# One kernel, one change: plain weight layout in the feed-forward part, mLSTM with carried states, and other groups and steps

## The chip, the cores and the metric

The kernel runs on one core of a Trainium2 chip. It is one launch; the metric is the device time of that launch in microseconds, taken as the median of three runs. A core has engines that each work through a queue of their own: TensorE (PE in the profile; its weight loads are listed as PEld), VectorE (DVE), ScalarE (ACT), GpSimd (POOL), and SyncE (SP), which here only issues DMAs.

## The reference

One encoder layer over 512 tokens of width 1024, with a memory of 256 tokens. All is fp32.

```python
h = rms_norm(x)
proj = h @ w_in       # q,k,v,o,gates of the mLSTM | q,k,v of attention B | q of attention C | 3 merge gates
A = mlstm_branch(...)                     # 4 heads of 128, forward and backward scan, summed
B = neighbourhood_attention(...)          # 8 heads of 64 on an 8 x 64 grid
C = memory_cross_attention(...)           # 4 heads of 128 into rms_norm(mem)
x = x + (g_ml * (A @ w_br_ml) + g_na * (B @ w_br_na) + g_xa * (C @ w_br_xa)) @ w_out
x = x + (gelu(dwconv3(a)) * u) @ w_down   # a, u = split(rms_norm(x) @ w_up), 2816 wide each
return rms_norm(x)
```

The mLSTM of one direction is linear attention with decay: a step keeps a state `C` (128 x 128) and a normaliser `n` (128) and does `C = decay * C + wt * v k^T`; within a chunk the scores are `exp(D) * q k^T`, and the result is scaled by `1 / max(|den|, exp(-m))`. The reference uses chunks of 64 tokens; any chunk length gives the same sums.

## The kernel before

**Products.** Activations stand channel by token: `XH`, `XL` hold the normalised input as a high part (rounded to the fast fp32r format) and the rest. A weight block is loaded raw by SP (`emit_raw`, L153, 512 KB), and split by `emit_split`: ACT copies it into the high half of a tile `w` (L213), DVE subtracts to get the low half (L214). `mm3` (L229 to L231) is high x high, high x low, low x high, so a *product* of one block (8 tiles of the contraction, 512 tokens) is 24 matmuls of 128x512. Each block is two `w` tiles; four `w` tiles exist, so ACT and DVE prepare the block after the one that PE is working on.

**Layout of w.** `layout` and `form` say where the high and low halves lie in a `w` tile. All blocks but two kinds have the plain layout, (1, 0, 0): high half from column 0, low half from column 512. The 44 blocks of the feed-forward's up projection (`ua`, `uu`) go through the 22 entries of `FORMS` in turn: shifted by 16, 32 or 48 floats; high and low interleaved (step 2) or interleaved by four (step 4) at several shifts; and eight in which the token axis is read and written backwards. `dn` blocks (down projection) are plain.

**Stages.** mLSTM q and k (`mlq`, `mlk`); then the token-major groups `tm` (tokens are the stationary side, the weights move): gates and half of v (272 columns), the other half of v (256), and attention B's v in two groups of 256; then products for C's q (`xaq`), the output gate (`o`), memory keys and values (`memk`, `memv`), B's q and k, three branches of eight merge gates with the branch projections, `out`, and twice up and down.

**Attention beside products.** The three mixers are generators (`ml_all`, `xa_all`, `na_all`), advanced by `step` after products at 1.4 steps a product (0.75 in the shorter memory products, `RATE` in the gates, half of it after the fourth contraction tile and half after the product). What `step` emits goes to the engines with the products around it. The order in which instructions then stand on each engine is fixed when the program is built, by a scheduler that may move one past another; on the chip each engine takes its own in that order.

**The mLSTM before.** `ml_prep` makes running gate sums (`lf`, scans over 512 tokens), the maxima `mr` and row biases, writes them to DRAM (`rd`, L546) and `load_R` reads them back, spread over all partitions: `R[d]` for direction d, 256 KB each (L576, SP), and `rm[d]`, the same plus a triangle mask (L579, POOL). Four buffers hold R and rm of one head. Per head, `kq_part` makes all 512 x 512 scores with four `mm3` (48 matmuls of 128x512 in all four heads) and ACT moves them to SBUF (L588). `weights_J` makes, for each 128-token block J of queries, five 128x128 tiles `exp(R + bias)` on ACT (L598) and multiplies them with the scores on DVE (L599, L600): one for each earlier key block (direction 0), each later one (direction 1) and the two diagonal ones. `values_J` multiplies them with `va` (v with a column of ones, 129 columns) on PE (L610): 80 plain fp32 matmuls, which the trace lists as 160, two for each. Then come the normaliser and the head's norm (L612 to L628).

## Time and profile before

| | |
|---|---|
| median of three runs | 899.22 us (898.06 to 899.22) |
| the profiled execution | 899.35 us, of which the span from the first to the last instruction is 897.6 us |
| 51.6 to 98.1 us | token-major groups |
| 98.1 to about 250 us | C's q, output gate, memory, B's q and k, with the mLSTM beside them |
| about 250 to 440 us | merge gates and branch projections, with attentions C and B beside them |
| 520.6 to 644.8 and 704.7 to 827.5 us | up projections, 22 products each |
| 644.8 to 704.7 us | first down projection |

A few rows in the prediction are read as follows. A page line such as `PE 888.7 (99%) x4438` is busy time, share of the span and number of instructions. A row of windows gives a stretch, its length, the busy time of each engine with the number of its instructions, the granted clock, and the DMA share. A row of the timeline gives the start, the length, the engine, line, operation and tiles, and in brackets how long the engine had been idle and what ended that. PE's matmuls overlap in the rows: 0.39 us is the modelled length of one, and the distance from one start to the next is what it costs.

### The profile page before, as it was taken

What the parts mean: (1) busy time and instruction counts of PE and PEld (TensorE: products, weight loads), DVE (VectorE), ACT (ScalarE), POOL (GpSimd) and SP (SyncE); (2) the same over time, 40 slices, a digit from 0 to 9 for tenths busy, and PEclk for the clock granted to TensorE, in tenths of its full rate; (3) what the DMA queues carried; (4) which work ended last, traced back from release to release, by engine and by line L of the source; (5) the groups of instructions that cost most, each with busy time, mean ns of one, the idle gap of its engine ahead of it and who ended that gap; (6) DMA issues with size and microseconds to landing.
All of it is one profiled execution on the core that took longest, in us unless ns stands there. A gap on an engine that the chain in (4) does not pass through costs nothing.

```text
span 897.6 us, 12396 instructions
## 1 busy us (share of the span) xinstructions
PE 888.7 (99%) x4438; PEld 758.9 (85%) x4438; DVE 599.7 (67%) x1138; ACT 467.6 (52%) x982; POOL 158.0 (18%) x236
## 2 busy tenths in 40 slices
PE   8999999999999999999999999999999999999997
PEld 7899888988888888888888888898888888988897
DVE  6795567747666757998766657677733577777433
ACT  7474446656544647898734435554422344544442
POOL 4201221112070660420000212111100011111010
PEclk9999999999999999999999999999999999999999
DMA  7323633532242443443323432322233322222312
GB/s 251 108 78 131 191 127 118 164 95 94 71 119 94 117 123 125 136 135 118 118 94 106 140 107 80 109 93 95 65 103 96 113 94 95 94 93 89 114 58 94
DMA packets 39437, 99.69 MB, mean 111 GB/s; under 512 B 5960, under 2 KB 13640, under 8 KB 39376
## 3 DMA queue, kind: packets, MB, share of 16 engines
q1 hardware_dynamic: 31728, 92.45, 31.6%
q0 software_dynamic: 7360, 6.32, 3.3%
q8 instruction: 35, 0.57, 0.2%
q14 instruction: 26, 0.21, 0.1%
q10 hardware_dynamic: 288, 0.14, 0.1%
HBM read 94.67 MB, written 4.21 MB: 110 GB/s over the span
## 4 chain that ended last, share of the span: by engine, by line
PE 93%; ACT 2%; DMA 2%; DVE 2%; issue 1%; SPq 0%; POOL 0%; POOLq 0%; ACTq 0%; DVEq 0%
PE mm L229 27%; PE mm L231 27%; PE mm L230 27%; PE at L229 2%; PE at L231 2%; PE at L230 2%; PE at L610 2%; PE at L755 1%; DMA R<-rd 1%; PE at L736 1%; DMA wr<-wflat 1%; DMA rd<-s 0%; PE at L843 0%; ACT s L727 0%; PE at L717 0%
## 5 line engine op out<-in xcount | busy, mean ns | idle before, releaser
L229 PE MATMUL mm<-u,w 128*128 128x512 f32 (+1 forms) x1077 | 418.7, 389 | 1.1 <-ACT w L213 0.8
L230 PE MATMUL mm<-u,w 128*128 128x512 f32 (+1 forms) x1077 | 416.2, 386 | 0.1
L231 PE MATMUL mm<-u,w 128*128 128x512 f32 (+1 forms) x1077 | 416.2, 386 | 0.0
L213 ACT ACTIVATE w<-wr 128x512 fp32r<-128x512 f32 (+1 forms) x290 | 181.9, 631 | 239.1 <-PE mm L231 207.0
L214 DVE TENSOR_TENSOR w<-wr,w 128x512 fp32r<-128x512 f32 (+3 forms) x291 | 220.8, 760 | 116.7 <-ACT w L213 113.4
L231 PEld LDWEIGHTS mm<-u,w 128*128 128x128 f32 x1077 | 207.7, 193 | 39.8 <-DVE w L214 0.4
L229 PEld LDWEIGHTS mm<-u,w 128*128 128x128 f32 x1077 | 207.8, 193 | 39.4 <-ACT w L213 1.3
L230 PEld LDWEIGHTS mm<-u,w 128*128 128x128 f32 x1077 | 207.8, 193 | 38.8 <-DVE u L236 0.8
L1171 POOL TENSOR_TENSOR s<-s,rb 128x512 f32<-128x512 f32 x22 | 30.6, 1392 | 265.2 <-DVE s L1170 256.6
L482 POOL DMA_DIRECT2D u<-nav_d x128 | 62.3, 501 | 73.3 <-PE at L755 33.6
L235 ACT ACTIVATE u<-s 128x512 fp32r<-128x512 f32 x34 | 21.4, 630 | 53.9 <-DVE s L1174 52.2
L236 DVE SCALAR_TENSOR_TENSOR u<-s,u 128x512 fp32r<-128x512 f32 x34 | 23.5, 691 | 14.9 <-ACT u L235 14.7
L598 ACT ACTIVATE E<-R,bi 128x128 f32<-128x128 f32 x80 | 27.9, 395 | 7.8 <-POOL R L579 3.8
L1017 POOL TENSOR_TENSOR acc<-acc,s 128x512 f32<-128x512 f32 x7 | 9.1, 1296 | 128.8 <-ACT s L1016 128.8
L400 ACT ACTIVATE s<-pad,vec 128x512 f32<-128x512 f32 x30 | 24.4, 812 | 6.9 <-DVE pad L398 6.6
L401 DVE SCALAR_TENSOR_TENSOR s<-pad,vec,s 128x512 f32<-128x512 f32 x30 | 22.5, 750 | 3.5 <-ACT s L400 2.6
L229 PE MATMUL mm<-w,u 128*128 128x256 f32 (+1 forms) x80 | 24.7, 308 | 0.0
L1170 DVE SCALAR_TENSOR_TENSOR s<-s,s 128x512 f32<-128x512 f32 x22 | 15.2, 692 | 14.0 <-ACT s L1169 14.0
L231 PE MATMUL mm<-w,u 128*128 128x256 f32 (+1 forms) x80 | 24.4, 305 | 0.0
L230 PE MATMUL mm<-w,u 128*128 128x256 f32 (+1 forms) x80 | 24.3, 304 | 0.0
L402 DVE SCALAR_TENSOR_TENSOR s<-pad,vec,s 128x512 f32<-128x512 f32 x30 | 22.5, 750 | 0.7
L1169 ACT ACTIVATE s<-s 128x512 f32<-128x512 f32 x22 | 13.9, 632 | 17.0 <-DVE s L1168 16.9
(276 smaller groups left out, 1066.7 us busy)
## 6 DMA issues: line engine op xcount, KB each, us to landing
wr<-wflat SPq DMA_DIRECT2D x140, 512.0 KB, 3.4
s<-xT SPq DMA_DIRECT2D x16, 256.0 KB, 4.1
nab<-nabias SPq DMA_DIRECT2D x16, 256.0 KB, 2.7
u<-nav_d POOLq DMA_DIRECT2D x128, 32.0 KB, 2.5
wr<-wflat SPq DMA_DIRECT2D x15, 192.0 KB, 2.4
nav_d<-nv POOLq DMA_DIRECT2D x8, 256.0 KB, 3.5
R<-rd SPq DMA_DIRECT2D x8, 256.0 KB, 3.6
wr<-wflat SPq DMA_DIRECT2D x2, 544.0 KB, 3.4
```

The source lines that it names most:

```text
L213: A.activation(h[:, u:v], src, AF.Copy)
L214: V.tensor_tensor(l[:, u:v], src, h[:, u:v].bitcast(F32), op=ALU.subtract)
L229: PE.matmul(ps, lh, rh, start=start, stop=False)
L230: PE.matmul(ps, lh, rl, start=False, stop=False)
L231: st["mm"] = PE.matmul(ps, ll, rh, start=False, stop=stop).ins
L236: V.scalar_tensor_tensor(l, src, scale, h.bitcast(F32), op0=ALU.mult, op1=ALU.subtract)
L400: A.activation(t1, pad[:, 0:512], AF.Identity, scale=vcol(w, i), bias=vcol(b, i))
L401: V.scalar_tensor_tensor(t1, pad[:, 1:513], vcol(w, n + i), t1, op0=ALU.mult, op1=ALU.add)
L402: V.scalar_tensor_tensor(t1, pad[:, 2:514], vcol(w, 2 * n + i), t1, op0=ALU.mult, op1=ALU.add)
L482: G.dma_start(vw[r * 32:(r + 1) * 32, i * 256:(i + 1) * 256], nav_v[hf, r, CW[b]:CW[b] + 32, hp * 256:(hp + 1) * 256])
L598: A.activation(E[:, i, :], src, AF.Exp, bias=bi[:, d, abs(J - s), s, h:h + 1])
L1171: G.tensor_tensor(c, c, rb2, op=ALU.mult)
```

## The change

There are five parts.

1. `FORMS`, `layout` and `form` go; every `w` tile has the plain layout. The new small tiles (`dg`, `ex`, `en`, less `tot` and the smaller `bi`) take 64 more fp32 columns ahead of the `w` tiles, 256 bytes.
2. Token-major groups are 272, 512 and 256 columns wide: the second half of v and the first half of B's v share one group.
3. The mLSTM goes by chunks of 128 tokens with carried states. q and k are kept as plain fp32, one unit buffer each (no split by `split_act`), and the unit buffers are 14 for 15. `keys` makes only the four diagonal score blocks of a head (plain fp32, 128x128), transposes the four key blocks, and scales them into `kt` (direction 0 on ACT, direction 1 on DVE). `states` multiplies three scaled key blocks per direction with v and adds them up into `C`. `diagonal` makes the eight diagonal exp tiles, `queries` the six scaled query tiles, and `values_J` adds one diagonal and one state matmul per direction. `load_R` of the next head is called two steps earlier. E tiles are six of 4 x 128 for two of 5 x 128.
4. `step` is called once after the eighth tile of a gate product and once after a branch projection.
5. Attention B's transposed weights use the same E tiles.

```diff
-NU = 15
+NU = 14
+EB = 6
 WARM = 13
 RM, RB = 0.75, 1.4
-RATE = (0.85, 1.05, 1.2)
+TMW = (272, 512, 256)
...
-FORMS = tuple((1, 16 * i, 0) for i in range(4)) + tuple((2, 8 * i, 0) for i in range(8)) + ((4, 0, 0), (4, 16, 0)) \
-    + tuple((1, 16 * i, 1) for i in range(4)) + tuple((2, 16 * i, 1) for i in range(4))
...
-            e = w[:, at:at + 2 * m].rearrange("p (j x) -> p x j", x=2)
-            h, l = e[:, 0, :], e[:, 1, :]
-        elif step == 4:
-            e = w[:, at:at + 2 * m].rearrange("p (y j z x) -> p x y z j", y=2, x=2, z=2)
-            h, l = e[:, 0], e[:, 1]
-            return h, l, [(h[:, k // 2, k % 2], l[:, k // 2, k % 2]) for k in range(4)]
-        else:
...
-                parts = [(h[:, k * c:(k + 1) * c], l[:, k * c:(k + 1) * c]) for k in range(b - a)]
             else:
-                step, at, _ = layout(key)
                 w = wp.tile([P, WT], F32R, tag="w", name=nm("w"), bufs=4)
-                h, l, parts = form(w, step, at, m, c)
+                h, l = w[:, :m], w[:, 512:512 + m] if m <= 512 else w[:, WT - m:]
...
-            split[i].extend(parts)
+            for k in range(a, b):
+                q = slice((k - a) * c, (k - a + 1) * c)
+                split[i].append((h[:, q], l[:, q]))
...
-            if layout(key)[2]:
-                mm3(ps[:, ::-1], ws[k][0], ws[k][1], XHs[k][:, ::-1], XLs[k][:, ::-1], k == 0, k == KT - 1)
-            else:
-                mm3(ps[:, :n], ws[k][0], ws[k][1], XHs[k], XLs[k], k == 0, k == KT - 1)
+            mm3(ps[:, :n], ws[k][0], ws[k][1], XHs[k], XLs[k], k == 0, k == KT - 1)
...
-        V.scalar_tensor_tensor(c, th, 1.0, c, op0=ALU.add, op1=ALU.mult)
-        split_act(dst[0][:, sl], dst[1][:, sl], c)
-    qT = [unit(F32R), unit(F32R)]
-    kT = [unit(F32R), unit(F32R)]
+        V.scalar_tensor_tensor(dst[:, sl], th, 1.0, c, op0=ALU.add, op1=ALU.mult)
+    qT, kT = unit(), unit()
...
+    for c, n in enumerate(TMW):
         pss = [(mmps if c % 2 else atps)() for _ in range(NT)]
-        for h in range(2):
+        g = 2 if n == 512 else 4
+        for h in range(KT // g):
             ws = weights(("tm", c, h))
             for t in range(NT):
                 tsl = slice(t * P, (t + 1) * P)
-                for k in range(4):
-                    kk = 4 * h + k
-                    ps = pss[t][:, :n]
-                    mm3(ps, XH[kk][:, tsl], XL[kk][:, tsl], ws[k][0], ws[k][1], kk == 0, kk == KT - 1)
+                for k in range(g):
+                    kk = g * h + k
+                    mm3(pss[t][:, :n], XH[kk][:, tsl], XL[kk][:, tsl], ws[k][0], ws[k][1], kk == 0, kk == KT - 1)
-            if c < 2:
-                A.activation(va[:, t, 2 * c:2 * c + 2, 0:128],
-                             ps[:, o:o + 256].rearrange("p (h c) -> p h c", h=2), AF.Copy, scale=rcc[:, t:t + 1])
+                to_va(0, t, ps[:, 16:272])
+            elif c == 1:
+                to_va(1, t, ps[:, :256])
+                to_nav(0, t, ps[:, 256:])
...
+                to_nav(1, t, ps[:, :256])
...
-        PE.matmul(pt[:, :32], ones, lf, start=True, stop=True)
+        PE.matmul(pt[:, :64], ones[:100], dg[:100].rearrange("p g t h -> p (g t h)"), start=True, stop=True)
...
+        mb = en[:, 0]
...
+        V.tensor_tensor(en[:, 1], en[:, 1], mb, op=ALU.subtract)
...
+            V.tensor_tensor(bi[:, d], gv[:, :, d, 0, :], pmv[:, :, 64 + 32 * d:68 + 32 * d], op=ALU.subtract)
+            V.tensor_tensor(ex[:, 0, d], bi[:, d], en[:, 1, d], op=ALU.add)
+            J, Jp = pr[d]
+            V.tensor_tensor(ex[:, 1, d, J], en[:, 1, d, J], mb[:, d, Jp], op=ALU.add)
+        A.activation(ex, ex, AF.Exp)
+        ml.update(rd=rd, em=em, bi=bi, mb=mb, ex=ex)
...
+        def etile():
+            return tp.tile([P, 4, P], F32, tag="E", name=nm("E"), bufs=EB)
+        def own(h):
+            u = unit()
+            return (u[:, 0:768].rearrange("p (d s c) -> p d s c", d=2, s=3),
+                    u[:, 768:1548].rearrange("p (d s c) -> p d s c", d=2, s=3))
+
+        def keys(h, kt):
+
+            kq, pt = atps(), atps()
+            hs = slice(h * S, (h + 1) * S)
+            for s in range(NT):
+                js, ss = slice(s * P, (s + 1) * P), slice(h * S + s * P, h * S + (s + 1) * P)
+                PE.matmul(kq[:, js], kT[:, ss], qT[:, ss], start=True, stop=True)
+            for s in range(NT):
+                PE.transpose(pt[:, s * P:(s + 1) * P], kT[:, h * S + s * P:h * S + (s + 1) * P], ident)
+            for i in range(3):
+                A.activation(kt[:, 0, i], pt[:, i * P:(i + 1) * P], AF.Copy, scale=ml["ex"][:, 0, 0, i, h:h + 1])
+                V.tensor_scalar(kt[:, 1, i], pt[:, (i + 1) * P:(i + 2) * P], ml["ex"][:, 0, 1, i + 1, h:h + 1], None,
+                                op0=ALU.mult)
+            return kq
+
+        def diagonal(h, p, rm, kq):
+
+            E = etile()
+            for i in range(4):
+                J, d = 2 * p + i // 2, i % 2
+                A.activation(E[:, i, :], rm[d][:, J * P:(J + 1) * P], AF.Exp, bias=bi[:, d, J, h:h + 1])
+            Ev = E.rearrange("p (j d) c -> p j d c", d=2)
+            kv = kq[:, 2 * p * P:(2 * p + 2) * P].rearrange("p (j c) -> p j c", j=2)
+            for d in range(2):
+                V.tensor_tensor(Ev[:, :, d], Ev[:, :, d], kv, op=ALU.mult)
             return E
-        def values_J(h, J, E, H, ss):
+        def queries(h, d, R):
+
+            t = etile()
+            J0 = 1 - d
+            for i in range(3):
+                J = J0 + i
+                A.activation(t[:, i, :], R[d][:, J * P:(J + 1) * P], AF.Exp,
+                             bias=mb[:, d, J - 1 if d == 0 else J + 1, h:h + 1])
+            V.tensor_tensor(t[:, 0:3], t[:, 0:3],
+                            qT[:, h * S + J0 * P:h * S + (J0 + 3) * P].rearrange("p (i c) -> p i c", i=3), op=ALU.mult)
+            return t
+
+        def states(h, kt, C):
+
+            for d in range(2):
+                ps = atps()
+                pv = ps[:, :390].rearrange("p (s c) -> p s c", s=3)
+                order = range(3) if d == 0 else range(2, -1, -1)
+                for i in order:
+                    PE.matmul(pv[:, i, 0:129], kt[:, d, i], va[:, i + d, h, 0:129], start=True, stop=True)
+                for n, i in enumerate(order):
+                    if n == 0:
+                        A.activation(C[:, d, i, 0:129], pv[:, i, 0:129], AF.Copy)
+                    else:
+                        V.scalar_tensor_tensor(C[:, d, i, 0:129], C[:, d, prev, 0:129], ml["ex"][:, 1, d, i + d, h:h + 1],
+                                               pv[:, i, 0:129], op0=ALU.mult, op1=ALU.add)
+                    prev = i
+        def values_J(h, J, E, Q, C, H, ss):
...
+                i = J - 1 if d == 0 else J
+                inter = 0 <= i < 3
+                PE.matmul(pv[:, d, 0:129], E[J // 2][:, 2 * (J % 2) + d, :], va[:, J, h, 0:129], start=True, stop=not inter)
+                if inter:
+                    PE.matmul(pv[:, d, 0:129], Q[d][:, i, :], C[:, d, i, 0:129], start=False, stop=True)
...
+            kt, C = own(h)
+            kq = keys(h, kt)
+            E = [diagonal(h, 0, rm, kq)]
...
+            states(h, kt, C)
+            E.append(diagonal(h, 1, rm, kq))
+            Q = [queries(h, d, R) for d in range(2)]
             yield
+            if h < 3:
+                R, rm = load_R(h + 1)
...
+            for J in range(NT):
+                values_J(h, J, E, Q, C, H, ss)
                 if J == 1 and prev:
                     emit_y(h - 1, prev[0])
                 yield
             prev = (H, ss)
...
-            ps = proj(("g", br, f), XH, XL, at={3: lambda: step(RATE[br] / 2)})
+            ps = proj(("g", br, f), XH, XL, at={KT - 1: step})
-            step(RATE[br] / 2)
...
-            step(RATE[br])
+            step()
```

The order of instructions changes most at the first head. On PE, before: behind the transposes of `mr` (L551) come the sum of `lf` and two score products of 3, then the output gate's first product.

```order
L551 MATMUL at_175_1344<-ident_117,s_159_1238 128x100 x4
L553 MATMUL at_176_1349<-lf_1179,ones_122 128x32
L229 MATMUL at_182_1373<-u_57_437,u_59_439 128x512
L230 MATMUL at_182_1373<-u_58_438,u_59_439 128x512
L231 MATMUL at_182_1373<-u_57_437,u_60_440 128x512
L229 MATMUL at_183_1378<-u_57_437,u_59_439 128x512
L230 MATMUL at_183_1378<-u_58_438,u_59_439 128x512
```

On PE now, the same place: the transposes (L537), the sum over `dg` (L539), the four diagonal scores (L586) and the four key transposes (L588) of head 0, and then the output gate's first product (24 rows with `mm_182`).

```order
L537 MATMUL at_169_1234<-ident_117,s_153_1120 128x100 x4
L539 MATMUL at_170_1239<-dg_1179,ones_122 128x64
L586 MATMUL at_176_1263<-u_57_437,u_58_438 128x128 x4
L588 MATMUL at_177_1264<-ident_117,u_58_438 128x128 x4
L203 MATMUL mm_182_1294<-u_8_148,w_164_1188 128x512
```

On PE behind that product now stand the six matmuls of `states` (L626, `u_175` is `kt` and `C` of head 0); behind the next product (24 rows with `mm_193`) and the column sums of the memory (L285) stand the first values (L642 with a diagonal tile, L644 with a state).

```order
L626 MATMUL at_185_1324<-u_85_573,u_175_1262 128x129 x3
L626 MATMUL at_186_1331<-u_85_573,u_175_1262 128x129 x3
L203 MATMUL mm_193_1363<-u_8_148,w_180_1288 128x512
L204 MATMUL mm_193_1363<-u_10_150,w_180_1288 128x512
L205 MATMUL mm_193_1363<-u_8_148,w_180_1288 128x512
```

Before, the six score matmuls needed only q and k; now what stands there needs tiles that ACT and DVE make.

On ACT, before: the row `em` (L555), one exp of head 0, two score copies (L588), and then the other exps, of masked rows (`R_178` and `R_180` are `rm[0]` and `rm[1]`) and of plain ones (`R_177`, `R_179`).

```order
L555 ACTIVATE em_1351<-at_175_1344 128x144
L598 ACTIVATE E_201_1477<-R_178_1366,bi_1355 128x128
L588 ACTIVATE u_181_1372<-at_182_1373 128x512
L588 ACTIVATE u_181_1372<-at_183_1378 128x512
L598 ACTIVATE E_201_1477<-R_180_1370,bi_1355 128x128
L598 ACTIVATE E_201_1477<-R_179_1368,bi_1355 128x128 x3
```

On ACT now: the exps of `diagonal` (L600; `R_172` and `R_174` are `rm[0]` and `rm[1]`) stand between the copies into `kt` (L590).

```order
L541 ACTIVATE em_1241<-at_169_1234 128x144
L600 ACTIVATE E_178_1279<-R_172_1256,bi_1245 128x128 x2
L553 ACTIVATE ex_1181<-ex_1181 128x64
L600 ACTIVATE E_178_1279<-R_174_1260,bi_1245 128x128
L590 ACTIVATE u_175_1262<-at_177_1264,ex_1181 128x128
L600 ACTIVATE E_178_1279<-R_174_1260,bi_1245 128x128
L600 ACTIVATE E_187_1338<-R_172_1256,bi_1245 128x128
L590 ACTIVATE u_175_1262<-at_177_1264,ex_1181 128x128
L600 ACTIVATE E_187_1338<-R_174_1260,bi_1245 128x128
L600 ACTIVATE E_187_1338<-R_172_1256,bi_1245 128x128
L590 ACTIVATE u_175_1262<-at_177_1264,ex_1181 128x128
```

A little further on ACT now: the query exps (L613), one half of a weight block (L185), exps of the next head's masked row (`R_198`, head 1), the other half, and only then the copies that begin the states (L629).

```order
L613 ACTIVATE E_188_1345<-R_171_1254,en_1243 128x128 x3
L613 ACTIVATE E_189_1350<-R_173_1258,en_1243 128x128 x3
L185 ACTIVATE w_191_1357<-wr_163_1186 128x512
L600 ACTIVATE E_233_1565<-R_198_1401,bi_1245 128x128 x2
L185 ACTIVATE w_192_1360<-wr_163_1186 128x512
L629 ACTIVATE u_175_1262<-at_185_1324 128x129
L934 ACTIVATE s_183_1319<-s_183_1319 128x512
L629 ACTIVATE u_175_1262<-at_186_1331 128x129
```

Every copy into `kt` on ACT now stands behind an exp of `rm[1]`, and both state copies stand behind exps of the next head's masked row.

117 lines of the change are left out of this document (38 added, 79 removed).

## The prediction

> **What bounds the kernel now.** I read the page's busy table and slices first, then the chain that ended last, then windows of single stages.
>
> ```profile
> span 897.6 us, 12396 instructions
> PE 888.7 (99%) x4438; PEld 758.9 (85%) x4438; DVE 599.7 (67%) x1138; ACT 467.6 (52%) x982; POOL 158.0 (18%) x236
> ...
> PEclk9999999999999999999999999999999999999999
> ...
> PE 93%; ACT 2%; DMA 2%; DVE 2%; issue 1%; SPq 0%; POOL 0%; POOLq 0%; ACTq 0%; DVEq 0%
> ```
>
> PE is busy for 888.7 of 897.6 us at full clock, and 93% of the chain is PE's own work. So the time is the number of PE's instructions times their distances, plus the few places where PE waits. A change counts if it alters that sum, or if it adds a wait. All sums below are made against the profiled execution, 899.35 us (span 897.6, the rest around it), which is 0.13 us above the median of 899.22.
>
> **Part 1, the layout of the up projection's weights.**
>
> ```profile
> 644.80:704.66 59.86, 59.86 (x266) 49.55 (x264) 23.11 (x34) 14.95 (x25) 1.29 (x1) 1.00 0.32 107
> 704.66:827.50 122.84, 122.84 (x529) 103.59 (x528) 91.87 (x120) 57.31 (x87) 13.28 (x10) 1.00 0.28 90
> 704.66:710.10 5.44, 5.44 (x26) 4.50 (x24) 2.05 (x3) 1.27 (x2) 0.00 (x0) 1.00 0.30 98
> 710.10:715.69 5.59, 5.59 (x25) 4.51 (x24) 4.15 (x6) 3.16 (x5) 0.00 (x0) 1.00 0.29 94
> 776.99:782.70 5.71, 5.71 (x25) 5.67 (x25) 4.97 (x8) 3.16 (x6) 0.00 (x0) 1.00 0.46 164
> ```
>
> The first row is a down projection, plain layout: 264 matmuls (count of the loads) in 59.86 us, 226.7 ns each. The second is an up projection: 528 in 122.84, 232.7 ns each. Same matmul, same full clock, no wait of PE in either. Inside the up projection the first product, the only one there with the plain layout, takes 5.44 us, the rate of the down projection; the next, shifted by 16 floats, takes 5.59, and one interleaved by four 5.71. So the layout sets the rate. Plain for all: 528 x (232.7 - 226.7) = 3.1 us, twice: **6.2 us** saved. DVE is busy 91.87 of 122.84 there, so it has room to feed the faster rate.
>
> The Trainium skill, "SBUF — State Buffer", section "Door 1: The DMA port swizzle (why `[64,N]` ≈ `[32,N]`)", speaks against this size: SBUF has 16-byte lines, and two fp32 hits a line suffice for full bandwidth, so shifts by whole lines and interleaving by two would be free. By it only the four products interleaved by four gain, 4 x (5.71 - 5.44) = 1.1 us. The 5.59 us of a product that is only shifted by 64 bytes says otherwise; I take the trace.
>
> **Part 2, token-major groups.**
>
> ```profile
> 40.75:51.63 10.88, 10.88 (x49) 9.01 (x48) 10.81 (x18) 6.92 (x12) 0.00 (x0) 1.00 0.30 99
> 63.58:86.61 23.03, 23.03 (x194) 23.03 (x193) 14.49 (x40) 12.30 (x25) 3.54 (x6) 1.00 0.31 104
> ```
>
> The first row is two products, 48 matmuls of 512 columns: 226.7 ns. The second is two groups of 256 columns: 192 matmuls in 23.03, 120 ns. Two narrow groups become one of 96 wide matmuls: 23.03 - 96 x 0.2267 = **1.3 us** saved. The evacuation of the wide group (ACT and DVE) lies under the 11.5 us of the group behind it; without that cover it would cost the first output product some of its own length, at most 5.4.
>
> **Part 3, the mLSTM's matmuls.**
>
> ```profile
> 127.83 0.39 PE L229 MATMUL at<-u,u 128*128 128x512 f32 x1
> ...
> 129.19 0.39 PE L229 MATMUL mm<-u,w 128*128 128x512 f32 x1
> ...
> 165.76 1.28 PE L610 MATMUL at<-u,E 128*128 128x129 f32 x10
> 166.88 0.60 PE L634 MATMUL at<-ident,H 128*128 128x128 f32 x4
> ```
>
> Six score matmuls go from 127.83 to 129.19: 0.227 each, 48 of them 10.9 us. They go. A plain fp32 matmul of 129 columns is listed as two: ten rows in 1.12 us up to the next start, so 0.224 a matmul; a transpose is (166.88 row) 0.11. The new 16 diagonal scores of 128 columns are not in the trace; the nearest row is this one, and I take it: 16 x 0.224 = 3.6, and 16 transposes x 0.11 = 1.8. As a bound, at the price of a 512-column matmul each they would cost the same 3.6; at half, 1.8. The values stay: 56 for 80 with E and state, and 24 in `states`, 80 in all, as before. Saved 10.9 - 5.4 = **5.5 us** (bounds 5.5 and 7.3).
>
> Sum of PE's work: 6.2 + 1.3 + 5.5 = 13.0 us.
>
> **What is late next.** The new matmuls of `states` need `kt`, which ACT scales, and ACT now stands first at an exp of `rm[1]`. In the rows of before:
>
> ```profile
> 120.39 0.51 PE L551 MATMUL at<-ident,s 100*128 100x100 f32 x4
> ...
> 121.64 0.35 SPq L576 DMA_DIRECT2D R<-rd  x1
> ...
> 128.26 1.29 POOL L579 TENSOR_TENSOR R<-R,msk 128x512 f32<-128x512 f32 x1 [2.24 <-DMA R<-rd]
> ...
> 129.59 1.57 ACT L598 ACTIVATE E<-R,bi 128x128 f32<-128x128 f32 x5 [2.15 <-POOL R L579]
> ...
> DMA to landing us min/median/max: 3.2/3.6/6.6
> ```
>
> SP reloads `R[1]` at 121.64, it lands at 128.2 (6.6 us, the longest of eight), POOL adds the mask, and ACT's exp of `rm[1]` starts at 129.59. Before, that hurt nobody: PE wanted the product of those tiles only at 135. Everything to here hangs on PE's place, so it moves up with part 2: 128.3 in the changed run. PE's arrival: the transposes end at 119.1 + 0.35; then the sum 0.2, keys 0.9 + 0.44, one product 5.44: **126.4**. From 128.3 ACT has eight instructions to the last `kt` (five exps, three copies; 1.57 for five is 0.3 each): 130.8. DVE's third scaled block follows one exp multiplied: about 131.1. Then 3 x 0.224: `states` ends at 131.8 instead of 126.4 + 1.3 = 127.7. **Wait: 4.1 us.** Behind it on PE stand all products.
>
> The second place is the first values, which need `C`. Their copies stand on ACT behind query exps, a weight half, two exps of the next head's `rm[0]`, and the other half:
>
> ```profile
> L598 ACT ACTIVATE E<-R,bi 128x128 f32<-128x128 f32 x80 | 27.9, 395 | 7.8 <-POOL R L579 3.8 <-DVE bi L565 3.5 <-DMA R<-rd 0.5
> L213 ACT ACTIVATE w<-wr 128x512 fp32r<-128x512 f32 x271 | 171.6, 636 | 216.8 <-PE mm L231 189.2 <-DMA wr<-wflat 10.2 <-PE at L231 7.0
> L616 ACT ACTIVATE H<-at,y 128x128 f32<-128x128 f32 x16 | 5.7, 358 | 1.4 <-DVE y L615 1.2
> L617 DVE SCALAR_TENSOR_TENSOR H<-at,y,H 128x128 f32<-128x128 f32 x16 | 5.6, 350 | 5.2 <-ACT H L616 5.0
> L906 ACT ACTIVATE s<-s 128x512 f32<-128x512 f32 x4 | 2.5, 634 | 1.5 <-DVE s L905 1.4
> ```
>
> The next head's `R[0]` goes into the buffer that ACT leaves at 130.5: landing 3.6 (median), mask 1.3, so its exps start at 135.4 and end at 136.1; weight half 0.64; copy 0.36; the gate's tanh 0.63; copy 0.36: 138.1; then three of DVE's additions at 0.35: **139.2**. PE comes there at 131.8 + 5.44 + 0.25 (column sums) + 0.45 (diagonal values) = 137.9. **Wait: 1.3 us** (4.3 if the reload takes 6.6). In the other heads I find the reload early enough: their rows are fetched a head ahead.
>
> The wait that stood here before goes:
>
> ```profile
> 135.00 0.47 PE L610 MATMUL at<-u,E 128*128 128x129 f32 x2
> 135.81 1.16 PE L610 MATMUL at<-u,E 128*128 128x129 f32 x8 [0.35 <-DVE E L600]
> ```
>
> Two halves take 0.22, and the next starts 0.81 later: 0.6 us. Net new waits: 4.1 + 1.3 - 0.6 = 4.8 us.
>
> **Costed at nothing.** Eight splits of q and k fewer (PE is busy throughout there), one unit buffer fewer, deeper E tiles, and steps at the ends of products:
>
> ```profile
> 22.00:60.00 38.00, 38.00 (x204) 32.99 (x203) 32.78 (x54) 19.71 (x33) 5.50 (x5) 1.00 0.30 99
> 350.00:400.00 50.00, 49.85 (x257) 41.80 (x256) 44.85 (x125) 43.00 (x115) 15.51 (x32) 1.00 0.47 138
> ```
>
> In the gates DVE (44.85) and ACT (43.00 of 50) nearly fill the time; a step is hidden by the product in front of it, and there are now 1 for 1.05 and 1.2 steps a product. If one dependent chain a branch came bare, it would be about a microsecond each.
>
> Forecast: 899.35 - 13.0 + 4.8 = 891.15, say **891.1 us**; with the reload slow 894.1.
>
> **The rivals.**
>
> *Nobody waits.* If `R[1]` lands in 3.6 instead of 6.6 us, the first wait shrinks to about a microsecond and the second goes; with less in ACT's way none is left: 899.35 - 13.0 - 0.6 = 885.7. For it: 6.6 is the longest of eight landings. Against it: the DMAs before it are the same, and ACT's order is fixed. 0.26.
>
> *The waits lower the clock.*
>
> ```profile
> 891.06 0.60 PE L1093 MATMUL at<-ident,u 128*128 128x128 f32 x4
> ...
> 894.00:896.00 2.00, 0.00 (x0) 0.99 0.72 262
> 896.00:897.60 1.60, 0.00 (x0) 0.50 0.00 0
> ```
>
> These are PE's last matmuls and two windows behind them (PE alone, then clock, DMA share, GB/s). PE idles from 891.7; the clock stands at 0.99 until 896 and at 0.50 behind. So idleness halves it, after some 4.3 us. If the wait at `states` does that, the product behind it runs at half rate, 10.9 for 5.44: 891.1 + 5.4 = 896.5. Against it: by ACT's order the first `kt` comes after one exp and a copy from 128.3, at 128.9, so the longest stretch with nothing is 2.5 us, and the matmuls of direction 0 break the rest. 0.08.
>
> The Trainium skill, "TensorE: Matmul & The Clock Gate", section "What's actually happening", has the clock fall to half after one idle window of about 3.4 us that runs freely; the trace's drop at 4.3 agrees. By that rule too a 2.5 us stretch leaves the clock alone, and a late reload, which makes it longer, would not.
>
> *Every head waits like the first.* This ends slower. In each head PE passes `keys`, then a product, then `states`, and ACT has exps of `rm` between. If the rows of heads 1 to 3 also land late, because a buffer of the four is free only when ACT has read the head before, the 4.1 + 1.3 = 5.4 us come four times: 899.35 - 13.0 - 0.6 + 4 x 5.4 = 907.4. It decides from 13.6 us of waits on, 3.4 a head. For it: the page's group of exps has idle time of ACT from late rows (7.8 behind POOL's mask). Against it: `load_R` of head h + 1 stands four steps, some three products (16 us), ahead of its `keys`, and landing and mask took 3.6 + 1.3. 0.07.
>
> *The layout isn't the cause.* If 232.7 ns comes from something else in the up projections (DVE is busy for 75% there, 39% in the down projection), part 1 gives nothing: 891.1 + 6.2 = 897.3. Against it: the 5.44 us product stands in the same stage, though as its first. 0.04.
>
> **How the numbers follow.** The forecast, 0.55, stands at 891.1, with the reload slow 894.1, and with the bound of the scores 889.3. Nobody waits, 0.26: 885.7, and with that bound 883.9. Clock 0.08, 896.5; layout 0.04, 897.3; every head 0.07, 907.4. A range from 884.0 to 896.5 leaves out the last two and the edge of the second. A measurement of this kernel can tell about 0.2%, 1.8 us, from no change. Only the last rival is slower: 0.07. The layout rival, 2.0 us below, is faster by a hair, close to that limit, so half of its chance, 0.02, goes to no change. Faster 0.91.
>
> **What would show it.** In the profile after: up projections at 5.44 us a product; 96 matmuls of the wide token-major group in 21.8 us; PE's busy time at 888.7 - 13.0, about 875.7; eight fp32 rows for four diagonal scores at 0.112 each. Before the first matmul of `states` PE idles some 3 to 4 us, released by ACT's copy into `kt`, and about 1.3 before the first value with a state; in the later heads there is none. The clock stays at 1.00. I am wrong in part 1 if those products stay near 5.6; wrong in the waits if `R[1]` lands in under 4 us or heads 1 to 3 wait too; wrong in part 3 if fp32 rows of 128 columns take longer than those of 129.

## The result, and the profile after

The changed kernel takes 888.52 us (median of four runs, 886.98 to 888.91) against 899.22; the ratio is 0.988, with a 95% interval from 0.9863 to 0.9897. The profiled execution took 888.33 us, 11.0 less than that of before. The forecast was 891.1, so the gain was foreseen at 8.2 us and came out at 11.0.

First the changed kernel's page: span, busy times, clock by slices, and the chain that ended last.

```profile
span 886.5 us, 12192 instructions
PE 875.3 (99%) x4342; PEld 741.6 (84%) x4342; DVE 580.3 (65%) x1153; ACT 449.8 (51%) x955; POOL 165.6 (19%) x238
...
PEclk9999999999999999999999999999999999999999
...
PE 94%; DMA 2%; DVE 1%; issue 1%; ACT 1%; POOL 0%; SPq 0%; POOLq 0%; DVEq 0%; ACTq 0%
```

PE is still the bound. Its busy time fell by 13.4 us, the span by only 11.1: some of the gain went into waits. Where the gain comes from is read from windows of equal work. These are windows of the kernel before: token-major groups; mLSTM (from the transposes of `mr` to the last transposes of a head); the gates with attention B beside them; first up projection.

```profile
51.63:98.13 46.50, 46.50 (x385) 46.49 (x384) 31.31 (x71) 24.65 (x46) 5.67 (x10) 1.00 0.39 125
120.39:252.15 131.76, 131.41 (x718) 113.34 (x716) 83.49 (x194) 79.00 (x225) 19.03 (x18) 1.00 0.34 108
338.06:444.43 106.37, 105.88 (x554) 89.66 (x553) 90.21 (x257) 88.34 (x233) 15.51 (x32) 1.00 0.41 124
520.61:644.80 124.19, 124.19 (x539) 104.86 (x538) 88.52 (x132) 59.09 (x91) 17.49 (x12) 1.00 0.29 92
```

And the same four of the changed kernel, with the second up projection at the end.

```profile
51.23:96.48 45.25, 45.25 (x289) 41.47 (x288) 27.63 (x64) 20.47 (x39) 5.99 (x10) 1.00 0.40 128
118.75:249.52 130.77, 127.02 (x718) 109.70 (x716) 84.62 (x212) 71.48 (x206) 19.52 (x18) 1.00 0.34 109
329.85:445.14 115.29, 115.29 (x601) 98.87 (x600) 94.71 (x264) 92.52 (x239) 31.05 (x64) 1.00 0.45 133
515.89:636.98 121.09, 121.09 (x540) 100.40 (x538) 82.96 (x132) 55.66 (x91) 19.33 (x12) 1.00 0.29 94
696.82:816.50 119.68, 119.68 (x530) 99.13 (x528) 81.70 (x120) 54.61 (x87) 18.09 (x10) 1.00 0.29 92
```

The up projections went from 124.19 and 122.84 us to 121.09 and 119.68: 6.3 us. The token-major groups gained 1.25. The mLSTM's window, with the same products in it, gained only 1.0, and PE sits idle in it for 3.75 us (130.77 less 127.02) where before it idled for 0.35. The window of attention B holds 360 matmuls of products before and 408 now; 48 more at 0.2267 us are 10.9, and the window grew by only 8.9, so 1.95 us went there; the prediction had nothing for it. The groups were not run by themselves: their window holds nothing else. These make 10.5 of 11.1; 0.4 more is the stretch ahead of the groups (51.63 and 51.23), and that is chance: in the profiles of the other runs the groups begin anywhere from 50.6 to 52.9 us.

The table of PE's waits in the changed kernel (who waited, for whom, us in total, times, the longest):

```profile
PE at L626 <- ACT u L590: 1.7, 3, 1.0
PE at L303 <- DVE s L302: 1.2, 1, 1.2
...
PE at L644 <- DVE u L631: 0.8, 1, 0.8
```

`states` (L626) and the first values (L644) were expected. L303, the matmul that spreads the memory's norm over the partitions, was not.

### The profile page after: what moved, and what is told of

Its sections match the earlier page's. It is cut to its first block, busy times and chain, and to the rows that moved or that the text cites. A ratio compares the mean times of both kernels' runs of the same rounds, so it can differ in the third digit from the quotient of the medians.

```text
span 886.5 us, 12192 instructions
## 1 busy us (share of the span) xinstructions
PE 875.3 (99%) x4342; PEld 741.6 (84%) x4342; DVE 580.3 (65%) x1153; ACT 449.8 (51%) x955; POOL 165.6 (19%) x238
## 4 chain that ended last, share of the span: by engine, by line
PE 94%; DMA 2%; DVE 1%; issue 1%; ACT 1%; POOL 0%; SPq 0%; POOLq 0%; DVEq 0%; ACTq 0%
PE mm L205 28%; PE mm L203 28%; PE mm L204 28%; PE at L203 2%; PE at L205 2%; PE at L204 2%; DMA R<-rd 1%; PE at L783 1%; PE at L764 1%; PE at L642 1%; PE at L644 1%; DMA s<-xT 1%; DMA rd<-s 0%; PE at L626 0%; PE at L745 0%
## 5 line engine op out<-in xcount | busy, mean ns | idle before, releaser
L185 ACT ACTIVATE w<-wr 128x512 fp32r<-128x512 f32 (+1 forms) x298 | 184.4, 623 | 239.7 <-PE mm L205 209.1
L186 DVE TENSOR_TENSOR w<-wr,w 128x512 fp32r<-128x512 f32 (+3 forms) x299 | 213.7, 716 | 114.4 <-ACT w L185 112.2
L205 PEld LDWEIGHTS mm<-u,w 128*128 128x128 f32 x1077 | 202.4, 188 | 40.8 <-DVE w L186 0.7
L203 PEld LDWEIGHTS mm<-u,w 128*128 128x128 f32 x1077 | 202.6, 188 | 39.6 <-ACT u L209 0.7
L204 PEld LDWEIGHTS mm<-u,w 128*128 128x128 f32 x1077 | 202.6, 188 | 39.2 <-DVE u L210 0.5
L1198 POOL TENSOR_TENSOR s<-s,rb 128x512 f32<-128x512 f32 x22 | 37.3, 1695 | 252.5 <-DVE s L1197 240.0
L209 ACT ACTIVATE u<-s 128x512 fp32r<-128x512 f32 x26 | 16.4, 631 | 55.3 <-DVE s L1201 54.5
L1201 DVE TENSOR_TENSOR s<-mm,s 128x512 f32<-128x512 f32 x22 | 15.2, 691 | 23.3 <-POOL s L1198 23.3
L210 DVE SCALAR_TENSOR_TENSOR u<-s,u 128x512 fp32r<-128x512 f32 x26 | 18.0, 691 | 14.7 <-ACT u L209 14.7
L203 PE MATMUL mm<-w,u 128*128 128x512 f32 x48 | 19.0, 395 | 0.0
L205 PE MATMUL mm<-w,u 128*128 128x512 f32 x48 | 18.7, 390 | 0.0
L204 PE MATMUL mm<-w,u 128*128 128x512 f32 x48 | 18.7, 390 | 0.0
```

What stands on the lines that cost most here:

```text
L185: A.activation(h[:, u:v], src, AF.Copy)
L186: V.tensor_tensor(l[:, u:v], src, h[:, u:v].bitcast(F32), op=ALU.subtract)
L203: PE.matmul(ps, lh, rh, start=start, stop=False)
L204: PE.matmul(ps, lh, rl, start=False, stop=False)
L205: st["mm"] = PE.matmul(ps, ll, rh, start=False, stop=stop).ins
L209: A.activation(h, src, AF.Copy, scale=scale)
```

## The experiments

Two of the parts put back, and the mLSTM put back, each alone.

**The layout of the weights.**

```diff
+                step, at, _ = layout(key)
...
-                h, l = w[:, :m], w[:, 512:512 + m] if m <= 512 else w[:, WT - m:]
+                h, l, parts = form(w, step, at, m, c)
...
```

> The changed kernel with the old layouts of the up projection's weights put back, nothing else. Theory (the layout sets PE's rate there): a product of an up projection goes from 5.44 us back to about 5.58 on average, 6.1 us in all, so 888.5 becomes 894.6. Rival (the slow rate came from what else stood beside those products): products stay at 5.44 and the time at 888.5. By the Trainium skill, page SBUF — State Buffer, section Door 1, only the four products interleaved by four would be slower, which is 1.1 us: 889.6.

Measured: 894.47 us (894.32 to 895.21). The windows of its two up projections:

```profile
515.61:639.80 124.19, 124.19 (x540) 104.84 (x538) 88.14 (x131) 59.12 (x91) 17.37 (x12) 1.00 0.27 91
699.65:822.50 122.85, 122.85 (x530) 103.58 (x528) 90.81 (x120) 57.27 (x87) 13.80 (x10) 1.00 0.27 90
```

124.19 and 122.85 us are those of the kernel before to 0.01 us. The layout alone sets this rate.

**The steps beside the gates.**

```diff
+RATE = (0.85, 1.05, 1.2)
...
-            ps = proj(("g", br, f), XH, XL, at={KT - 1: step})
+            ps = proj(("g", br, f), XH, XL, at={3: lambda: step(RATE[br] / 2)})
...
+            step(RATE[br] / 2)
...
-            step()
+            step(RATE[br])
```

> The changed kernel with the old steps in the gates (0.85, 1.05 and 1.2 a product, half of them after the fourth contraction tile). Theory (half steps in the middle of a product made PE wait in attention B and split its runs): about 2.0 us more, 890.5, and waits of PE at the products with the transposed weights come back, some 1.5 us. Rival (the six smaller E buffers took those waits away): no change, 888.5.

Measured: 890.48 us (890.16 to 891.41). Its window of attention B, and then three rows of the same stage in the kernel before (start, length):

```profile
336.45:442.79 106.34, 105.84 (x554) 89.65 (x553) 90.16 (x257) 88.32 (x233) 31.09 (x64) 1.00 0.45 134
```

```profile
419.36 0.40 PE L755 MATMUL at<-w,u 128*128 128x256 f32 x2
...
419.62 0.42 DVE L744 TENSOR_TENSOR w<-at,w 128x256 fp32r<-128x256 f32 x1
...
420.10 0.52 PE L755 MATMUL at<-w,u 128*128 128x256 f32 x2 [0.34 <-DVE w L744]
```

The window is that of before again, 106.34 with 360 product matmuls, with the six new E buffers in place. So it was the steps, and not the buffers. The rows show how: with half steps in mid-product, PE comes to the attention's values (L755) while DVE is still making the split weights for them (419.62 + 0.42), and waits 0.34 us. With whole steps a product of 5.4 us stands between.

PE's idle time is only 0.5 us in this window, before and with the steps put back, where the expectation had 1.5. The rest of the 1.95 us lies between starts, in time that is listed as busy. In the kernel before the weight loads (PEld) of this stage wait as well:

```profile
PEld at L755 <- DVE w L744: 1.6, 4, 0.6
...
PEld at L736 <- ACT s L730: 0.8, 3, 0.4
```

The run with the old steps has the same two waits at its own lines, 1.6 and 0.8 us; in the changed kernel's window no weight load waits. From start to start, the 64 matmuls of L755 take 8.69 us before and 7.63 in the changed kernel, which is 1.06 of the 1.95; most of what is left is at the products. The edit sets two things at once, how many steps there are and where in a product they stand; no run here separates them.

**The old mLSTM, with the three other parts.** The kernel before with the plain layout, the groups of 272, 512 and 256 and the whole steps.

```diff
-RATE = (0.85, 1.05, 1.2)
+TMW = (272, 512, 256)
...
-                step, at, _ = layout(key)
...
-                h, l, parts = form(w, step, at, m, c)
+                h, l = w[:, :m], w[:, 512:512 + m] if m <= 512 else w[:, WT - m:]
...
-            ps = proj(("g", br, f), XH, XL, at={3: lambda: step(RATE[br] / 2)})
+            ps = proj(("g", br, f), XH, XL, at={KT - 1: step})
```

> The kernel before with three parts of the change (plain layout, groups of 272, 512 and 256, whole steps) and the old mLSTM. Theory (the carried-state mLSTM is worth only about 1 us net: about 5 of PE's work less, 4.0 of waits more, and 0.7 of old wait less by the two traces): 889.5. Rival (it is the larger part of the gain, the prediction's 5.5 of work without waits): 893 or more. If the waits cost more than the work saves: below 888.5.

Measured: 889.98 us (888.99 to 890.52). Windows of its mLSTM and of attention B:

```profile
120.07:251.16 131.09, 131.09 (x717) 113.26 (x716) 84.10 (x193) 78.49 (x224) 19.18 (x18) 1.00 0.33 109
331.49:446.79 115.30, 115.30 (x602) 98.87 (x600) 94.71 (x264) 92.50 (x239) 20.86 (x43) 1.00 0.42 128
```

The gain in attention B is here too, so it has nothing to do with the mLSTM. The old mLSTM takes 131.09 us and PE never idles in it; the new one, in the changed kernel, 130.77 with 3.75 idle. Of the whole change, the largest edit in the diff is worth about 1.5 us as it stands, by the medians; the intervals of the two ratios overlap (0.9884 to 0.9913 here, 0.9863 to 0.9897 for the changed kernel), so even that is not clear of the noise.

**The waits.** In the first head of the changed kernel, this is how `states` comes to wait. SP's issue of the reload and POOL's row, then ACT's and PE's; the last row is the product behind `states`:

```profile
120.47 0.35 SPq L564 DMA_DIRECT2D R<-rd  x1
...
125.16 1.41 POOL L567 TENSOR_TENSOR R<-R,msk 128x512 f32<-128x512 f32 x1 [0.54 <-DMA R<-rd]
...
126.60 0.40 ACT L600 ACTIVATE E<-R,bi 128x128 f32<-128x128 f32 x1 [1.10 <-POOL R L567]
126.91 0.35 ACT L590 ACTIVATE u<-at,ex 128x128 f32<-128x128 f32 x1
...
127.31 0.49 PE L626 MATMUL at<-u,u 128*128 128x129 f32 x2 [1.00 <-ACT u L590]
128.14 0.49 PE L626 MATMUL at<-u,u 128*128 128x129 f32 x2 [0.34 <-ACT u L590]
128.98 1.40 PE L626 MATMUL at<-u,u 128*128 128x129 f32 x8 [0.35 <-ACT u L590]
130.13 0.47 PE L203 MATMUL mm<-u,w 128*128 128x512 f32 x1
```

The copy into `kt` at 126.91 needs nothing that is late, but it stands behind the exp that waits for the mask. And this is the unexpected wait at L303:

```profile
140.62 1.31 POOL L567 TENSOR_TENSOR R<-R,msk 128x512 f32<-128x512 f32 x1 [5.44 <-DMA R<-rd]
141.88 1.06 POOL L289 TENSOR_TENSOR rc_m<-y,nhalf 128x2 f32<-128x2 f32 x1
...
142.97 0.20 ACT L296 ACTIVATE y<-rc_m 128x2 fp32r<-128x2 f32 x1 [0.89 <-POOL rc_m L289]
...
144.57 1.14 ACT L185 ACTIVATE w<-wr 128x512 fp32r<-128x512 f32 x2
...
145.22 0.69 DVE L186 TENSOR_TENSOR w<-wr,w 128x512 fp32r<-128x512 f32 x1 [0.99 <-ACT w L185]
145.83 0.68 DVE L933 TENSOR_TENSOR s<-mm,rb_x 128x512 f32<-128x512 f32 x1
146.43 0.67 DVE L302 TENSOR_SCALAR s<-ident,y 128x128 fp32r<-128x128 f32 x3
...
146.96 0.39 PE L303 MATMUL at<-s,onesr 128*128 128x256 f32 x1 [1.25 <-DVE s L302]
```

Read from the top: POOL has the mask of a later head's row ahead of the memory's small power (L289), and waits 5.44 us for that row's reload. So the power is late; ACT's rounding of it (L296) is late, ACT's weight halves (L185) behind it too, then DVE's (L186), DVE's evacuation (L933), the small diagonal tile (L302), and PE at last. Four queues, each in its fixed order, carry one late reload to PE.

The first experiment changes the order of issue of the first head alone: its diagonal exps (L600) go behind its copies into `kt` (L590). `ka` is the last of these copies, which `keys` now returns too; `issue_after` sets the order of issue.

```diff
...
+            kq, ka = keys(h, kt)
+            with tc.issue_after(ka) if h == 0 else nullcontext():
+                E = [diagonal(h, 0, rm, kq)]
...
+            with tc.issue_after(ka) if h == 0 else nullcontext():
+                E.append(diagonal(h, 1, rm, kq))
```

> The changed kernel with the exps of the first head's diagonal tiles issued behind its three copies into kt on ACT (order of issue alone). Theory (PE's wait at states comes from the copies standing behind exps of the masked row, and the first values' wait from the state copies standing behind exps of the next head): the 2.2 us before the six matmuls of states fall to under 0.4, the 1.1 us at the first values fall to under 0.3, and the wait of 1.4 us at the memory's row sum (L303 in the changed kernel) stays, since GpSimd still has the third head's mask ahead of the small power: about 885.5. Rival (the copies are late because ex itself, or the transposes, are late): the wait at states stays near 2 us, 888.5.

Measured: 886.95 us (886.31 to 889.04). Its rows of `states` and of L303, and then three windows: PE's wait before L303, a stretch behind it, and the one that follows (the clock is the third number from the end):

```profile
125.53 1.50 PE L626 MATMUL at<-u,u 128*128 128x129 f32 x12
...
143.86 0.39 PE L303 MATMUL at<-s,onesr 128*128 128x256 f32 x1 [2.55 <-DVE s L302]
```

```profile
141.31:143.86 2.55, 0.00 (x1) 0.00 (x1) 1.74 (x5) 1.71 (x5) 0.00 (x0) 1.00 0.00 0
144.81:148.23 3.42, 3.42 (x12) 2.83 (x11) 1.50 (x5) 1.55 (x6) 1.18 (x1) 0.50 0.46 153
148.34:152.00 3.66, 3.66 (x23) 3.20 (x22) 1.60 (x3) 1.76 (x6) 0.36 (x1) 1.00 0.00 0
```

Both expected waits are gone: the twelve rows of `states` follow one another with no bracket. But the wait at L303 grew from 1.25 to 2.55. Counted from the transposes of `mr`, PE came there 3.8 us earlier than in the changed kernel (at 141.31 with the transposes at 118.13, for 145.71 and 118.75), and the mask that POOL has ahead of the small power only 2.5 us earlier (137.54 and 140.62). The expectation had kept that wait as it was.

It also missed what the longer wait did. About a microsecond behind it the granted clock fell to 0.50 and stayed there for 3.4 us. From L303 to the eighth matmul of the next product are 4.48 us here and 2.90 in the changed kernel, so this cost 1.6 us, more than the wait had grown. The mean clock of all four executions of this version is 0.996 or 0.997, that of the changed kernel 0.998 to 1.00, so it was likely there in each. In the end this version's window from the transposes to the last transposes of a head is 129.89 us for 130.77: of what the edit won, 0.9 us is left. The ratio to the kernel before, 0.9869 (0.9854 to 0.9884), is not clear of the changed kernel's.

The second does it for every head. Then the next heads' exps no longer run early, their rows' buffers come free later, and POOL's power stands ahead of the mask.

```diff
...
+            kq, ka = keys(h, kt)
+            with tc.issue_after(ka):
+                E = [diagonal(h, 0, rm, kq)]
...
+            with tc.issue_after(ka):
+                E.append(diagonal(h, 1, rm, kq))
```

> As the run with the first head alone, but the diagonal exps of every head are issued behind that head's copies into kt. This also puts GpSimd's power for the memory's norm ahead of the third head's mask. Theory (the wait at the memory's row sum comes from that mask, which waits for a reload): all three waits go, 4.7 us in all: 883.8. Rival (later heads now wait, since their exps can no longer be done early): the first head's gain is given back at states or values of heads 1 to 3, and the time is 886 or more. Second rival (the wait at the row sum comes from the weight copies on ACT): 885.3.

Measured: 885.37 us (883.65 to 886.31). The window of its mLSTM, then POOL's power, which now waits for DVE and no longer for a reload, and L303:

```profile
119.90:246.58 126.68, 126.04 (x718) 109.48 (x716) 86.51 (x212) 70.73 (x206) 20.41 (x18) 1.00 0.35 113
```

```profile
137.47 1.11 POOL L289 TENSOR_TENSOR rc_m<-y,nhalf 128x2 f32<-128x2 f32 x1 [1.30 <-DVE y L287]
...
143.72 0.38 PE L303 MATMUL at<-s,onesr 128*128 128x256 f32 x1 [0.64 <-DVE s L302]
```

The window fell from 130.77 to 126.68, by 4.1 us, and no later head gave anything back. 0.64 of wait is left at L303, from what is further down the chain, the weight halves ahead of the evacuation and the small tile. The time fell by 3.1 and not by 4.7. Besides those 0.6, the 4.7 were taken from the first profile of the changed kernel, which has more waiting than its repetition below: against that one's window of 129.35 the edit is worth 2.7 us.

The next two runs move the memory's row of norms (L296 to L305) one product later, in the changed kernel and together with the edit before. A third runs the changed kernel again beside them.

```diff
-        if f == 2:
+        if f == 3:
             mrb = rstd_row(mrc, M, "m")
```

> The changed kernel with the memory's row of norms made one product later (after the fourth output-gate product instead of the third). Theory (the 1.4 us that PE waits at the first of its two matmuls is a wait for a small tile of DVE that stands behind late weight copies, so a place with six more matmuls ahead of it hides it): that wait goes, the waits at states and first values stay, and PE's time beside the plain matmuls in the mLSTM's stage falls from 32.2 us to about 30.8; the time to about 887.1. Rival (the late row only moves the wait to the same matmul, since the tile follows the product's evacuation there too): 888.5 and the same wait.

> Both edits: diagonal exps behind the copies into kt in every head, and the memory's row one product later. Theory: the last 0.6 us of wait in the mLSTM's stage goes; its time beside the plain matmuls falls from 28.1 to 27.5 us, and the time from 885.4 to 884.8. Rival (something else becomes late at the later place, such as the memory keys' evacuation that needs the row): 885.4 or more.

> The changed kernel once more, unedited, on the chip of the two runs beside it, to compare them with it directly. 888.5 within 1 us; its waits at states, first values and the memory's row sum together 3.5 to 5 us, and no change in attention B (22.8 us beside the plain matmuls).

Measured: 886.83 us (885.68 to 889.13), 884.66 (882.83 to 885.02) and 888.37 (886.79 to 888.80). The windows of the mLSTM, in that order:

```profile
119.88:248.18 128.30, 126.89 (x717) 109.77 (x716) 83.65 (x212) 70.44 (x205) 19.59 (x18) 1.00 0.34 111
```

```profile
120.37:246.18 125.81, 125.81 (x717) 109.54 (x716) 85.44 (x212) 70.57 (x205) 21.20 (x18) 1.00 0.36 114
```

```profile
119.83:249.18 129.35, 126.97 (x718) 109.72 (x716) 84.56 (x212) 70.50 (x205) 19.24 (x18) 1.00 0.33 110
```

With the row alone moved, the wait at L303 is gone and those at `states` and the first values stay (0.9 and 0.5 us), as expected. With both edits PE is busy for all of the window's 125.81 us. That version beats both kernels: 0.9834 of the kernel before (0.9820 to 0.9848), where the changed kernel on the same chip is at 0.9880 (0.9866 to 0.9894). The changed kernel run again has 2.4 us of idle PE in this window where its first profile had 3.75, and where 3.5 to 5 were expected. What differs is how far PE is when a reload lands: PE's transposes stood at 118.75 in the first profile and at 119.83 in the repetition, but SP issued the first reload at 119.54 and 119.62. It follows the writing of the rows (POOL's DMA into `rd`), which took 4.2 us to land in the first and 3.2 in the second. So PE's earlier start was lost again in waits: `states` ended at 130.13 in both.

**Which shifts cost.** The last two runs put the up projection's weights at other start addresses, one shift a product, the other product of each pair plain.

```diff
+SHIFT = (0, 64, 48, 32, 16, 8, 4, 2, 1, 24, 40)
...
-                h, l = w[:, :m], w[:, 512:512 + m] if m <= 512 else w[:, WT - m:]
+                at = SHIFT[key[1] % HF] if key[0] == "ua" else 0
+                ah = at if key[0] == "ua" and key[1] < HF else 0
+                h, l = w[:, ah:ah + m], w[:, 512 + at:512 + at + m] if m <= 512 else w[:, WT - m:]
```

> The changed kernel; the first projection of each up pair has its high and low halves shifted by 0, 64, 48, 32, 16, 8, 4, 2, 1, 24 and 40 floats, in that order, in the first half of the products, and the low half alone in the second half. Theory 1 (what counts is whether a weight block of 512 bytes starts on a multiple of 256 bytes): 0 and 64 take 5.44 us a product, all others about 5.55 to 5.6; with the low half alone shifted a third of the excess. Theory 2 (lines of 16 bytes, from the Trainium skill, page SBUF — State Buffer, section Door 1): all shifts by a multiple of 4 floats take 5.44, and only 1 and 2 could be slower. Theory 3 (the excess grows with the shift modulo 64): 16 slowest of the multiples of 16, as 5.59 us in the kernel before, then 32, then 48.

```diff
+SHIFT = (12, 20, 28, 36, 44, 52, 60, 56, 6, 3, 5, 4, 8, 16, 32, 48, 40, 24, 64, 0, 2, 1)
...
+                at = SHIFT[key[1]] if key[0] == "ua" else 0
+                h, l = w[:, at:at + m], w[:, 512 + at:512 + at + m] if m <= 512 else w[:, WT - m:]
```

> The map of shifts again, both halves shifted, in other places: 12, 20, 28, 36, 44, 52, 60, 56, 6, 3, 5 in the first half of the up projection, 4, 8, 16, 32, 48, 40, 24, 64, 0, 2, 1 in the second. Theory (the start address of the weights alone sets the rate): 4, 64 and 0 take 5.44 us again, 8, 16, 24, 32, 40, 48, 2 and 1 take 5.50 to 5.62 again, although they stand at other places. Rival (what stands beside a product sets it): the repeated shifts change places. Of the odd multiples of four, either all are as fast as 4 (5.44) or 4 is alone in that.

Measured (24 matmuls, from the start of the first to the start of the next product's first, both halves shifted; 20 is left out, since other matmuls stood in its product, and 12 is worked out from the 21 matmuls of its product that stand together):

| shift, floats | us a product |
|---|---|
| 0, 3, 4, 36, 60, 64 | 5.44 |
| 48, 44 | 5.49, 5.52 |
| 2, 6 | 5.54, 5.55 |
| 52, 1 | 5.57 |
| 32, 28, 5, 56, 8, 12, 16, 40, 24 | 5.59 to 5.61 |

Four windows of the second map, one product each: shifts of 4, 8 and 64 floats, then of 48.

```profile
698.35:703.79 5.44, 5.44 (x26) 4.50 (x25) 2.05 (x3) 1.27 (x2) 0.00 (x0) 1.00 0.28 98
709.23:714.83 5.60, 5.60 (x26) 4.51 (x24) 3.37 (x5) 1.93 (x4) 1.81 (x1) 1.00 0.29 97
775.49:780.93 5.44, 5.44 (x26) 4.50 (x25) 3.33 (x5) 1.94 (x4) 1.81 (x1) 1.00 0.28 96
```

```profile
742.38:747.87 5.49, 5.49 (x25) 4.51 (x24) 3.37 (x5) 1.95 (x4) 1.81 (x1) 1.00 0.28 96
```

A shift that stood in both runs, at other places in the program, took the same time to 0.01 us wherever no other matmul stood between the products: the address sets it, not the neighbours. But none of the three theories holds. Shifts by a multiple of 256 bytes are free, as theory 1 says, yet 4, 3, 36 and 60 floats are free too. Lines of 16 bytes don't explain 8 and 16, and the excess is no function of the shift that grows or falls. With the low half alone shifted (a third of the weight loads) the products of shift 8, 16 and 32 took 5.59, 5.54 and 5.55, which is two thirds of the excess or all of it and not a third; at 48 it took 5.55, more than with both halves shifted. What in the chip makes it is open.

## Why the prediction came out as it did, step by step

The changed kernel's profiled execution stands beside the prediction's sum; the mLSTM's work is from the two runs in which PE never idled there (131.09 old, 125.81 new).

| step | predicted, us | measured, us |
|---|---|---|
| plain layout | -6.2 | -6.3 |
| token-major groups | -1.3 | -1.25 |
| mLSTM, PE's work | -5.5 | -5.3 |
| mLSTM, new waits | +5.4 | +5.0 (130.77 less 125.81); +3.5 in the repetition |
| mLSTM, old wait gone | -0.6 | -0.7 (131.76 less 131.09) |
| steps beside the gates | 0 | -1.95 |
| start and the rest | 0 | -0.6 |
| sum | -8.2 | -11.1 (span) |

**The layout** was right in mechanism and size, and shown by putting it back. The rule of the Trainium skill (SBUF — State Buffer, Door 1) that the prediction weighed against its own row would have had 1.1 us here; 6.3 were measured, and shifts by whole 16-byte lines cost up to 0.17 us a product. The row of the trace was the better guide. That the rate depends on more than "shifted or not" could not be seen from the layouts of before.

**The mLSTM's work** was right to 0.2 us; the nearest rows (plain fp32 of 129 columns, two rows of 0.112) held for the new scores of 128.

**The old wait** went by about the forecast amount, but not for the forecast reason alone. The run with the old mLSTM has no idle PE in this window either. There the same reload landed in 5.4 us, where the profile of before had 6.6.

**The new waits** came near in sum, and that was partly luck: a part that was too large met one that wasn't foreseen, and in the repetition the sum is 3.5. In distances from start to start, `states` cost 2.7 us more than in the run with all exps behind the copies, where nothing waits there, and 1.6 more in the repetition; 4.1 were predicted. The step that was mis-sized is the reload of `R[1]`, taken at 6.6 us from the profile before. In the changed kernel the landing times of the eight reloads are:

```profile
DMA to landing us min/median/max: 3.0/3.8/4.6
```

The longest, 4.6, is again that of `R[1]` in the first head (issued at 120.47, POOL's mask at 125.16). It is the longest of the eight in eleven of the twelve profiles: 6.6 us before, 5.4 in the run with the old mLSTM, and 4.3 to 4.9 with the carried states. So the prediction was right that the long landing belongs to this place, and its size was wrong by 2 us; what shortened it is open. Behind the reload the working held: from ACT's exp of the masked row to the end of `states` it has 3.5 us (128.3 to 131.8), and the rows show 3.5 (126.60 to 130.13). The rival "nobody waits" had a landing of 3.6; at 4.6 the waits were shorter but did not go. The mechanism, copies behind exps of a masked row, was shown by changing the order alone.

The first values waited 0.8 us (1.3 predicted), and their wait went with the same edit. Beside them stands a wait that the prediction didn't have, 1.25 us at L303: it had followed POOL's queue for the masks of the first head, but not for the small power that now stands behind a mask of a later head, because rows come free earlier and their masks move up in POOL's order. Heads 1 to 3 did not wait at `states`, as forecast.

**The clock** stayed at 1.00 in the changed kernel, where PE's longest idle stretch in the mLSTM is 1.25 us. But the reason for the rival's small chance does not hold. The prediction took a stretch of 2.5 us as harmless, on two grounds, one of them a drop that came 4.3 us behind PE's last work; the measurement goes against both. In the run with the first head's exps moved, 2.55 us without work were followed by a clock of 0.50. At the end of the twelve profiles the drop comes 2.1 to 5.1 us behind PE's last matmul, so one such time is no threshold. Had the wait at `states` been as long as forecast, the clock might have fallen; that it didn't is in part luck. The price was too high as well: 5.4 us in the prediction, 1.6 in that run.

**The steps** are the step that failed, as far as one did: "a step is hidden by the product in front of it" and was costed at nothing. In the changed kernel PE never idles in that stage; but the old steps did cost something. With them PE waited inside attention B, 0.34 us at the row shown, its weight loads waited 2.4 us, and its runs of products were split more often. The table of PE's waits of before had it, in the stage of attention B:

```profile
PE at L755 <- DVE w L744: 0.3, 1, 0.3
```

So had the stage's window, in which PE was busy for 105.88 of 106.37 us; the prediction took a part of it, with 49.85 of 50.00, and read it as full. These two show only 0.5 of the 1.95 us; the waits of the weight loads, quoted above, and the distances show the rest. 1.95 of the 2.8 us between forecast and result are from here; the rest is the start and smaller waits.

## What to carry to other kernels

Where one engine is busy for 99% of the time, count its instructions by their start-to-start distance in windows of equal work, before and after: here that gave four of the terms to 0.2 us. Before a removed part is costed at nothing, ask what it costs now: the old order's short waits hide in a busy time that is modelled. And a late transfer reaches the bounding engine through every in-order queue that has an instruction waiting for it; to take it out, move the ones that don't need it ahead, and look in the same place again, since the next wait takes over what is gained too early. One wait of 2.5 us can cost more than several of a microsecond with the same sum, as the clock showed here.

## What the runs showed of the hardware that was not expected

The rate of the same 128x512 fp32r matmuls depends on the start address of their weights in a way that repeats exactly and follows no simple rule: 226.7 ns each at shifts of 0, 3, 4, 36, 60 and 64 floats, up to 233.9 ns at 24, though the loads keep their length (4.50 us of them in the window of 5.44, 4.51 in that of 5.60). Behind some of the shifted products (16, 24 and 40, but not 8 or 56) the first few plain matmuls still run with uneven distances (233, 236, 224, 231, 236, 228, 233, 231 ns behind the shift of 40 in the first map) before the plain 227 returns, as if loads and matmuls had to fall back into step. That is a reading of the pattern; no run here tests it.

The clock fell to half behind an idle stretch of only 2.55 us (run with the first head's exps moved: PE without work from 141.31 to 143.86, granted clock 0.50 from 144.81 to 148.23). Stretches of up to 1.3 us inside the other runs left it at 1.00. No run here has one between these two lengths, so where the limit lies is open.
